# The projection of v and the second product of g in native float32

## The chip, the cores and the metric

One core of a Trainium2 chip runs the kernel. The metric is the device time of one execution in microseconds (us), as the median of several runs. Beside the timed runs there is one profiled execution, and all rows below come from it.

## The reference, cut to what matters

The kernel computes two layers, each a token mixer and a SwiGLU feed-forward network with post-normalisation, on x of 256 tokens by 1024 channels in float32. The first mixer is an RWKV-7 time mixing; the change touches v and g in it:

```
xx = time_shift(x) - x
xr, xw, xk, xv, xa, xg = [x + xx * mu[n] for n in range(6)]
r, k, v = xr @ w_r, xk @ w_k, xv @ w_v        # 256x1024 @ 1024x1024
g = sigmoid(xg @ g1) @ g2                     # g1: 1024x160, g2: 160x1024
...
S = S * w_t + (S @ -kk_t) b_t^T + v_t k_t^T   # per head and token
y_t = S @ r_t
y = group_norm(y) * gn_g + gn_b + bonus * v
return (y * g) @ w_o
```

The recurrence over tokens is done in four chunks of 64 tokens: the scores within a chunk, the inverse of a triangular matrix of each head and chunk, then four dependent steps (z, u, s, y) from chunk to chunk.

## The kernel before, in words

Most products are made from split parts. A weight piece of 128x1024 is loaded into a raw buffer (three of them in a ring), ScalarE (ACT) casts it to float32r as its high part (`hi`), and VectorE (DVE) or GpSimd (POOL) subtracts that from the raw piece to get the low part (`lo`); `PL` names the pieces whose subtraction is on POOL. The activations are split likewise (`xhi`, `xlo`). A product is then three matmuls: hi by xhi, lo by xhi, hi by xlo. `Stream` does this for every weight in the order of `weight_specs`; a piece of kind "native" is loaded into a slot of its own and used as float32 without a split (the first two pieces of k and both of g1), "stack" splits into one tile whose row groups hold hi, hi and lo, and "keep" leaves the parts in slots. All weight loads are issued by SyncE (SP), in that order.

In the first layer PE computes k, then r, then the scores (`sc`) of the chunks, the transposed keys (`bkt`), the bonus sums, the first half of v's columns, g1 and g2, and v's second half. v has the activations as the stationary side and 512 columns of the weights as the moving side: two halves of columns by two halves of tokens by 8 pieces of channels, 32 products. v's second half is cut into 16 units of one product. FREE = 10 of them run as they can; the rest are handed out one by one as fills for PE, four inside `merge` (counts in FILLI), and the last two in the recurrence (`fill`).

xv and xg are mixed on POOL (MIXV, MIXG), as two multiplications and additions on 128x512 for each quarter. xv is then split, by casts on ACT and subtractions on POOL ("xxv" in OFF); xg isn't, as g1 is native. The sigmoid of g's first product, `hg`, is split on ACT and DVE: three row groups, so that g2 takes four matmuls of 256 columns for each 128 channels, on stacked copies of the last 32 rows.

`inverse` runs on DVE: four transposes LT<-SC, a loop of 31 steps in which each product (`tmp<-LT,TT`) and addition (`TT<-TT,tmp`) needs the one before, then transposes TN and SC<-TT. `merge` multiplies the blocks on PE (n, t) with copies on ACT in between, and `recurrence` starts with z.

The order of the work is made in the program by `Issue`, a list of parts with ranks that are run against modelled times (`Clock`), and then by the framework's scheduler on each engine. After the mixer come the output projection, the networks and the attention, whose weights run through the same stream.

Of the kernel before, what the change touches and what calls it, by code (L numbers as in the profile page):

```python
# [8 lines left out]
F32 = mybir.dt.float32  # L9
# [7 lines left out]
T = 256  # L17
# [48 lines left out]
BON = 'pool'  # L66
BONW = 'T'
ORDERED = False
PL = {'wo1': [5, 6, 7], 'in1': [0, 1, 2, 3], 'qkv': [1, 3, 4, 5, 6, 7, 11], 'wo0': [1, 2, 4, 6, 7, 9, 10], 'k': [2], 'r': [0], 'v': [2, 3, 4, 5, 6, 7], 'g2': [0, 1], 'w2': [], 'in0': [0, 2, 3, 5]}
LD = {}  # L70
MIXV = 'pool'
MIXG = 'pool'
# [25 lines left out]
ORDER = mybir.DependencyInfo(mybir.DependencyClass.NoSync, mybir.DependencyReason.DATA)  # L98


class Stream:


# [8 lines left out]
        self.used = [Event() for _ in range(len(specs) + 1)]  # L112

    def load(self, upto):
        while self.nl < len(self.specs) and (self.nl < upto or self.specs[self.nl][1] == "native"):
            i = self.nl
            name, kind, a, b, rows, src = self.specs[i]
            if kind == "native":
                raw = self.slot([1024], f"nat{i}")
            else:  # L120
                raw = self.wp.tile([128, 1024], F32, tag="raw", name=f"raw{i}", bufs=RAW)
            v = raw[:rows, :a * b].rearrange("p (a b) -> p a b", a=a)
            if kind != "native":
                self.ring.append(i)
                if len(self.ring) > RAW:
                    self.I.clk.floor = max(self.I.clk.floor, self.freed.get(self.ring[-RAW - 1], 0.0))
            self.sync.dma_start(v, src.rearrange("p (a b) -> p a b", a=a))
            self.raw[i] = v
            self.nl += 1

    def run(self):
        for i, (name, kind, a, b, rows, src) in enumerate(self.specs):
            if i > 0 and self.specs[i - 1][1] == "raw":
                yield self.used[i]
            self.load(i + RAW)
            lead = self.lead.get(i, SPL - 1)
            if i >= lead:
                yield self.used[i - lead]
            r = self.raw.pop(i)
            if kind in ("native", "raw"):  # L140
                self.sp[i] = r
                self.I.reach(self.split[i], r)
                continue
            hl = []
            for t in ("hi", "lo")[:1 if kind in ("stack", "cast") else 2]:
                if kind in ("keep", "cast"):
                    x = self.slot([1024], f"{t}{i}", F32R)
                else:
                    x = self.wp.tile([128, 1024], F32R, tag=t, name=f"{t}{i}", bufs=SPL)
                hl.append(x[:rows, :a * b].rearrange("p (a b) -> p a b", a=a))  # L150
            if kind in ("split", "stack") and i >= SPL:
                yield self.done[i - SPL]
            if i in self.hold:
                yield self.hold[i]
            if name in self.gates:
                yield self.gates[name]
            yield r
            if kind in ("stack", "cast"):
                (self.pool.tensor_copy if kind == "cast" else self.act.copy)(out=hl[0], in_=r)
                yield hl[0]  # L160
                x = slice(rows // 3 * 2, rows)
                if kind == "stack":
                    (self.pool if i in self.pooled else self.dve).tensor_tensor(hl[0][x], r[x], hl[0][x].bitcast(F32), ALU.subtract)
                self.freed[i] = self.I.clk.ready(hl[0])
                self.sp[i] = hl
                self.I.reach(self.split[i], hl[0])
                continue
            n = 2 if name == "wo0" else 1
            c = b // n
            for j in range(n):  # L170
                self.act.copy(out=hl[0][:, :, j * c:(j + 1) * c], in_=r[:, :, j * c:(j + 1) * c])
                yield hl[0][:, :, j * c:(j + 1) * c]
                (self.pool if i in self.pooled else self.dve).tensor_tensor(hl[1][:, :, j * c:(j + 1) * c], r[:, :, j * c:(j + 1) * c],
                                       hl[0][:, :, j * c:(j + 1) * c].bitcast(F32), ALU.subtract)
            self.freed[i] = self.I.clk.ready(hl[1])
            self.sp[i] = hl
            self.I.reach(self.split[i], hl[1])
# [194 lines left out]
def weight_specs(a):  # L372
# [3 lines left out]
    def s1(name, key, idx, kind="split", cols=128):  # L376
        specs.append((name, kind, KT, cols, 128, a[key][idx]))

    def s2(name, key, cb, kind="split"):
        for q in range(4):  # L380
            specs.append((name, kind, 2, 512, 128, a[key][cb * 4 + q]))
# [18 lines left out]
            specs.append(("sel", "cast", KT, 128, 48, a["selT"]))  # L400
    for p in range(KT):
        s1("r", "w_r", p)
    s2("v", "w_v", 0)
    s1("g1", "w_g1a", 0, "native")
    s1("g1", "w_g1b", 0, "native", 96)
    specs.append(("g2", "split", 1, 1024, 128, a["w_g2a"]))
    specs.append(("g2", "stack", 1, 1024, 96, a["w_g2b"]))
    s2("v", "w_v", 1)
    s2("wo0", "w_o0", 0)
    s2("wo0", "w_o0", 1, "keep")  # L410
    s2("wo0", "w_o0", 0)
# [11 lines left out]
def trunk(ctx, tc, a, out):  # L423
# [23 lines left out]
    def slot(shape, name, dtype=F32):  # L447
        return tp.tile([128] + shape, dtype, tag="t4", name=nm(name))
# [4 lines left out]
    def half_slot(name, dtype=F32):  # L453
        return sm.tile([128, 2, T], dtype, tag="w2", name=nm(name), bufs=6)
# [4 lines left out]
    def ev(name):  # L459
        return E.setdefault(name, Event())  # L460
# [9 lines left out]
    def mm(ps, lhsT, rhs, start, stop, **kw):  # L470
        pe.matmul(ps, lhsT, rhs, start=start, stop=stop, **kw)
# [726 lines left out]
    def v_part(ps, w, hf, q, kks=(0, 1)):  # L1198
        for kk in kks:
            k = q * 2 + kk  # L1200
            xh, xl = mixed["xv"][k // 4]
            for n, (ww, xx) in enumerate(((w[0], xh), (w[1], xh), (w[0], xl))):
                mm(ps, xx[:, k % 4, TOK[hf]], ww[:, kk, :], start=(k + n == 0), stop=(k + n == KT + 1))

    def v_done(hf, cb, ps):
        act.copy(out=vt[hf][:, cb * 512:(cb + 1) * 512], in_=ps)
# [4 lines left out]
        I.reach(ev(f"v{cb}{hf}"), vt[hf][:, cb * 512:(cb + 1) * 512],  # L1211
                *(x[:, :, cb * 4:cb * 4 + 4] for x in UV[2 * hf:2 * hf + 2]))

    hgs = slot([3, T], "hg", F32R)

    def gates(n, rows, ps):

        yield ps[:rows, :T]
        x = half_slot("sg")[:rows, 0, :]
        act.activation(x, ps[:rows, :T], AF.Sigmoid)  # L1220
        yield x
        act.copy(out=hgs[:rows, n * 2, :], in_=x)
        yield hgs[:rows, n * 2, :]
        if n == 0:
            dve.tensor_tensor(hgs[:, 1, :], x, hgs[:, 0, :].bitcast(F32), ALU.subtract)
        else:
            dve.tensor_tensor(hgs[32:64, 2, :], x[32:64], hgs[32:64, 2, :].bitcast(F32), ALU.subtract)
        I.reach(ev(f"hg{n}"), hgs[:rows, n:n * 2 + 1, :] if n else hgs[:, 0:2, :])

    def g_done(u, ps):  # L1230
        act.copy(out=gT[u // 2][:, (u % 2) * 2:(u % 2) * 2 + 2, :], in_=a2(ps))
# [3 lines left out]
    def dense0():  # L1235
# [30 lines left out]
        for q in range(4):  # L1266
            ps = bank("r")
            for j in range(2):
                w = yield from W.get("r")
                yield from mm_s1(ps[:, j * T:(j + 1) * T], w, mixed["xr"])  # L1270
            I.add(3, receptance(q, ps))
            if q == 2:
                mix(3, "xv", 3, slot, eng=dict(pool=pool, dve=dve)[MIXV])
        early.close()
        scp = l0.enter_context(tc.tile_pool(name="scp", bufs=1))
        SC = scp.tile([128, 2, KT, NC, 128], F32, name="SC")
# [10 lines left out]
        for hf in range(2):  # L1287
            I.after(ps[hf], v_done, hf, 0, ps[hf])
        yield ev("xg")
        for n, rows in enumerate((128, 96)):  # L1290
            w = yield from W.get("g1")
            ps = bank("g1")
            for k in range(KT):
                mm(ps[:rows, :T], w[:, k, :], mixed["xg"][k // 4][:, k % 4, :], start=(k == 0), stop=(k == KT - 1))
            I.add(1, gates(n, rows, ps))
            yield 0.0
# [4 lines left out]
        for u in range(4):  # L1301
            ps = bank("g")
            for j in range(2):
                p = u * 2 + j
                for n, (ww, xx_) in enumerate(((g2[0][0], hgs[:, 0, :]), (g2[0][1], hgs[:, 0, :]), (g2[0][0], hgs[:, 1, :]),
                                               (g2[1][0], hgs[:96, 2, :]))):
                    mm(ps[:, j * T:(j + 1) * T], ww[:, 0, p * 128:(p + 1) * 128], xx_, start=(n == 0), stop=(n == 3))
                yield 0.0
            I.after(ps, g_done, u, ps)
        ws = []  # L1310
# [377 lines left out]
def _layout(inp):  # L1688
# [3 lines left out]
    def s1(w, n=128):  # L1692
        return w.reshape(KT, 128, w.shape[1] // n, n).transpose(2, 1, 0, 3).reshape(w.shape[1] // n, 128, KT * n)
# [10 lines left out]
    d["w_r"], d["w_k"], d["w_v"] = s1(rkv[0]), s1(rkv[1]), s2(rkv[2])  # L1704
    d["w_1"] = np.concatenate([inp["rwkv_w1"][0], inp["rwkv_a1"][0]], axis=1).reshape(2, 4, 128, 128).transpose(0, 2, 1, 3).reshape(2, 128, 512)
    d["w_2"] = np.stack([np.concatenate([w, w], axis=0) for w in (inp["rwkv_w2"][0], inp["rwkv_a2"][0])])
    d["w_g1a"], d["w_g1b"] = s1(inp["rwkv_g1"][0][:, :128]), s1(np.tile(inp["rwkv_g1"][0][:, 128:], (1, 3)), 96)
    d["w_g2a"], d["w_g2b"] = inp["rwkv_g2"][0][:128], np.tile(inp["rwkv_g2"][0][128:], (3, 1))
    d["w_o0"], d["w_o1"], d["w_qkv"] = s2(inp["rwkv_w_o"][0]), s2(inp["moba_w_o"][0]), s2(inp["moba_w_qkv"][0])
    for i in range(2):  # L1710
        w = inp["ffn_w_in"][i].reshape(KT, 128, 2, NJ, 128).transpose(3, 2, 1, 0, 4)
# [30 lines left out]
```

## Time and profile before

| | before |
|---|---|
| runs | 755.3, 751.78, 755.85 us; median 755.3 |
| profiled execution | 752.51 us, span from first to last instruction 750.7 us |
| mean granted PE clock | 0.963 |
| busy: PE, DVE, ACT, POOL | 692.8, 512.6, 359.3, 185.0 us |
| DMA | 117.27 MB, mean 156 GB/s |
| shares of the chain that ended last | PE 66%, DVE 10%, DMA 2% |

Times in rows are in us from the start of the span, durations of single instructions in ns where the view says so. PE is the matmul side of TensorE and PEld its weight loads. A matmul's duration in the rows is longer than the distance to the next one, because matmuls are pipelined; the distance between starts is what a matmul costs in a sequence. The granted clock of a stretch is a share of 2.4 GHz, so that 0.5 stands for 1.2 GHz. Nearly all instructions carry line 300, that of a helper, so that rows are told apart by their tiles. A native float32 matmul of the program stands as two instructions in the rows.

### The profile page before, as it was taken

To read this page: it belongs to the slowest core of one execution; us is meant where nothing else is said; L and a number is where in the kernel's file an instruction comes from. 1 tells how busy PE (TensorE), PEld (TensorE's weight loads), DVE (VectorE), ACT (ScalarE), POOL (GpSimd) and SP (SyncE) were. 2 spreads that over 40 slices of the span, in tenths; PEclk is the share of its full clock that TensorE was granted. 3 is DMA by queue.
4 is the path that set the end of the run, shared out by engine and by line. 5 is a ranking of instruction groups with operands and counts; after the bars stand their busy time and mean duration, and the time that the engine had idled before them with its cause. 6 is when DMAs were issued, how large, how long until landed. Compare 5 with 4: busy or idle time off the path is not lost.

```text
span 750.7 us, 12852 instructions
## 1 busy us (share of the span) xinstructions
PE 692.8 (92%) x5140; PEld 620.0 (83%) x5140; DVE 512.6 (68%) x827; ACT 359.3 (48%) x591; POOL 185.0 (25%) x132
## 2 busy tenths in 40 slices
PE   6899795798789999999999799999979999999996
PEld 5899784677668999999999578777769999999995
DVE  7989989938897655455555945876685554554566
ACT  5873234356545444434446314756635444444450
POOL 5667973333373000000000623113040000000000
PEclk9999998779999999999999989999999999999998
DMA  6445312110566655555557615445055555565551
GB/s 240 151 143 188 101 62 85 57 58 31 186 196 194 213 183 194 176 191 189 179 193 219 209 49 169 140 141 196 29 169 191 175 195 187 180 195 177 189 169 56
DMA packets 33580, 117.27 MB, mean 156 GB/s; under 512 B 3809, under 2 KB 4833, under 8 KB 33521
## 3 DMA queue, kind: packets, MB, share of 16 engines
q1 hardware_dynamic: 31936, 110.89, 45.3%
q10 hardware_dynamic: 1584, 5.57, 2.4%
q8 instruction: 40, 0.66, 0.4%
q14 instruction: 20, 0.16, 0.1%
HBM read 115.40 MB, written 1.05 MB: 155 GB/s over the span
## 4 chain that ended last, share of the span: by engine, by line
PE 66%; DVE 10%; DMA 2%; ACT 1%; issue 1%; DVEq 0%; ACTq 0%
PE gu L300 30%; PE acc L300 14%; PE qkv L300 9%; DVE xtok L300 4%; PE o L300 3%; PE gn L300 2%; DMA raw<-in_w_qkv_dram 2%; PE v L300 1%; PE tr L300 1%; DVE sc L300 1%; PE n L300 1%; PE ptr L300 1%; PE pv L300 1%; DVE lo L300 1%; PE att L300 1%
## 5 line engine op out<-in xcount | busy, mean ns | idle before, releaser
L300 DVE TENSOR_TENSOR lo<-raw,hi 128x1024 fp32r<-128x1024 f32 (+1 forms) x172 | 209.9, 1225 | 162.7 <-ACT hi L300 162.5
L300 ACT CAST hi<-raw 128x1024 fp32r<-128x1024 f32 (+1 forms) x214 | 212.4, 1001 | 209.1 <-PE gu L300 83.1
L300 PE MATMUL gu<-xhi,hi 128*128 128x256 f32 x640 | 181.1, 283 | 0.0
L300 PE MATMUL gu<-xlo,hi 128*128 128x256 f32 x640 | 181.0, 283 | 0.0
L300 PE MATMUL gu<-xhi,lo 128*128 128x256 f32 x640 | 180.9, 283 | 0.0
L300 POOL TENSOR_TENSOR lo<-raw,hi 128x1024 fp32r<-128x1024 f32 (+1 forms) x41 | 88.4, 2172 | 260.0 <-ACT hi L300 255.4
L300 PEld LDWEIGHTS gu<-xhi,hi 128*128 128x128 f32 x640 | 121.7, 190 | 0.7
L300 PEld LDWEIGHTS gu<-xhi,lo 128*128 128x128 f32 x640 | 121.7, 190 | 0.7
L300 PEld LDWEIGHTS gu<-xlo,hi 128*128 128x128 f32 x640 | 121.7, 190 | 0.0
L300 PE MATMUL acc<-hi,hl 128*128 128x512 f32 (+1 forms) x180 | 53.7, 368 | 0.0
L300 PE MATMUL acc<-lo,hh 128*128 128x512 f32 (+1 forms) x180 | 53.6, 367 | 0.0
L300 PE MATMUL acc<-hi,hh 128*128 128x512 f32 (+1 forms) x180 | 53.5, 367 | 0.0
L300 PE MATMUL qkv<-hi,xhi 128*128 128x512 f32 x96 | 40.6, 423 | 2.4 <-ACT xhi L300 2.4
L300 ACT CAST hh<-silu 128x256 fp32r<-128x256 f32 x40 | 16.2, 406 | 49.4 <-DVE silu L300 49.4
L300 PE MATMUL qkv<-lo,xhi 128*128 128x512 f32 x96 | 39.6, 412 | 0.0
L300 PE MATMUL qkv<-hi,xlo 128*128 128x512 f32 x96 | 39.6, 412 | 0.0
L300 PEld LDWEIGHTS acc<-hi,hl 128*128 128x128 f32 x180 | 32.8, 188 | 5.9
L300 PEld LDWEIGHTS acc<-lo,hh 128*128 128x128 f32 x180 | 32.7, 188 | 5.7
L300 PEld LDWEIGHTS acc<-hi,hh 128*128 128x128 f32 x180 | 31.8, 189 | 4.6
L300 PE MATMUL o<-hi,xhi 128*128 128x512 f32 x64 | 27.2, 425 | 3.0 <-ACT xhi L300 3.0
L300 DVE TENSOR_TENSOR hl<-silu,hh 128x256 fp32r<-128x256 f32 x40 | 17.0, 425 | 17.4 <-ACT hh L300 17.4
L300 PE MATMUL o<-hi,xlo 128*128 128x512 f32 x64 | 26.4, 415 | 0.0
(225 smaller groups left out, 1289.3 us busy)
## 6 DMA issues: line engine op xcount, KB each, us to landing
raw<-in_w_in_dram SPq DMA_DIRECT2D x80, 512.0 KB, 3.5
raw<-in_w_dn_dram SPq DMA_DIRECT2D x44, 512.0 KB, 3.5
raw<-in_w_qkv_dram SPq DMA_DIRECT2D x24, 512.0 KB, 3.9
raw<-in_w_o_dram SPq DMA_DIRECT2D x20, 512.0 KB, 3.6
raw<-in_w_r_dram SPq DMA_DIRECT2D x8, 512.0 KB, 3.9
raw<-in_w_v_dram SPq DMA_DIRECT2D x8, 512.0 KB, 3.5
raw<-in_w_if_dram SPq DMA_DIRECT2D x8, 512.0 KB, 3.4
raw<-in_w_k_dram SPq DMA_DIRECT2D x6, 512.0 KB, 3.8
```

What stands on the lines that cost most here:

```text
L300: ins = f(*args, **kw).ins
```

## The change

The four pieces of v's first half stay in the raw ring as loaded ("raw"); the four of its second half and the two of g2 are loaded straight into buffers of the rings that hold hi and lo parts ("in lo", "in hi"). xv is mixed into plain float32 tiles and not split. hg is written by the sigmoid alone. Each product of v becomes one native float32 matmul instead of three, each of g2 two (128 and 32 rows) instead of four. The last 32 rows of g1 and g2 are no longer repeated three times.

```diff
--- before.py
+++ after.py
@@ -66,7 +66,7 @@
 BON = 'pool'
 BONW = 'T'
 ORDERED = False
-PL = {'wo1': [5, 6, 7], 'in1': [0, 1, 2, 3], 'qkv': [1, 3, 4, 5, 6, 7, 11], 'wo0': [1, 2, 4, 6, 7, 9, 10], 'k': [2], 'r': [0], 'v': [2, 3, 4, 5, 6, 7], 'g2': [0, 1], 'w2': [], 'in0': [0, 2, 3, 5]}
+PL = {'wo1': [5, 6, 7], 'in1': [0, 1, 2, 3], 'qkv': [1, 3, 4, 5, 6, 7, 11], 'wo0': [1, 2, 4, 6, 7, 9, 10], 'k': [2], 'r': [0], 'in0': [0, 2, 3, 5]}
 LD = {}
 MIXV = 'pool'
 MIXG = 'pool'
@@ -98,6 +98,9 @@
 ORDER = mybir.DependencyInfo(mybir.DependencyClass.NoSync, mybir.DependencyReason.DATA)
 
 
+NATIVE = ("native", "in hi", "in lo")
+
+
 class Stream:
 
 
@@ -112,15 +115,17 @@
         self.used = [Event() for _ in range(len(specs) + 1)]
 
     def load(self, upto):
-        while self.nl < len(self.specs) and (self.nl < upto or self.specs[self.nl][1] == "native"):
+        while self.nl < len(self.specs) and (self.nl < upto or self.specs[self.nl][1] in NATIVE):
             i = self.nl
             name, kind, a, b, rows, src = self.specs[i]
             if kind == "native":
                 raw = self.slot([1024], f"nat{i}")
+            elif kind in NATIVE:
+                raw = self.wp.tile([128, 1024], F32R, tag=kind[3:], name=f"nat{i}", bufs=SPL).bitcast(F32)
             else:
                 raw = self.wp.tile([128, 1024], F32, tag="raw", name=f"raw{i}", bufs=RAW)
             v = raw[:rows, :a * b].rearrange("p (a b) -> p a b", a=a)
-            if kind != "native":
+            if kind not in NATIVE:
                 self.ring.append(i)
                 if len(self.ring) > RAW:
                     self.I.clk.floor = max(self.I.clk.floor, self.freed.get(self.ring[-RAW - 1], 0.0))
@@ -137,7 +142,7 @@
             if i >= lead:
                 yield self.used[i - lead]
             r = self.raw.pop(i)
-            if kind in ("native", "raw"):
+            if kind in NATIVE + ("raw",):
                 self.sp[i] = r
                 self.I.reach(self.split[i], r)
                 continue
@@ -400,12 +405,12 @@
             specs.append(("sel", "cast", KT, 128, 48, a["selT"]))
     for p in range(KT):
         s1("r", "w_r", p)
-    s2("v", "w_v", 0)
+    s2("v", "w_v", 0, "raw")
     s1("g1", "w_g1a", 0, "native")
-    s1("g1", "w_g1b", 0, "native", 96)
-    specs.append(("g2", "split", 1, 1024, 128, a["w_g2a"]))
-    specs.append(("g2", "stack", 1, 1024, 96, a["w_g2b"]))
-    s2("v", "w_v", 1)
+    s1("g1", "w_g1b", 0, "native", 32)
+    specs.append(("g2", "in hi", 1, 1024, 128, a["w_g2a"]))
+    specs.append(("g2", "in hi", 1, 1024, 32, a["w_g2b"]))
+    s2("v", "w_v", 1, "in lo")
     s2("wo0", "w_o0", 0)
     s2("wo0", "w_o0", 1, "keep")
     s2("wo0", "w_o0", 0)
@@ -1198,9 +1203,7 @@
     def v_part(ps, w, hf, q, kks=(0, 1)):
         for kk in kks:
             k = q * 2 + kk
-            xh, xl = mixed["xv"][k // 4]
-            for n, (ww, xx) in enumerate(((w[0], xh), (w[1], xh), (w[0], xl))):
-                mm(ps, xx[:, k % 4, TOK[hf]], ww[:, kk, :], start=(k + n == 0), stop=(k + n == KT + 1))
+            mm(ps, mixed["xv"][k // 4][:, k % 4, TOK[hf]], w[:, kk, :], start=(k == 0), stop=(k == KT - 1))
 
     def v_done(hf, cb, ps):
         act.copy(out=vt[hf][:, cb * 512:(cb + 1) * 512], in_=ps)
@@ -1211,21 +1214,13 @@
         I.reach(ev(f"v{cb}{hf}"), vt[hf][:, cb * 512:(cb + 1) * 512],
                 *(x[:, :, cb * 4:cb * 4 + 4] for x in UV[2 * hf:2 * hf + 2]))
 
-    hgs = slot([3, T], "hg", F32R)
+    hgs = slot([2, T], "hg")
 
     def gates(n, rows, ps):
 
         yield ps[:rows, :T]
-        x = half_slot("sg")[:rows, 0, :]
-        act.activation(x, ps[:rows, :T], AF.Sigmoid)
-        yield x
-        act.copy(out=hgs[:rows, n * 2, :], in_=x)
-        yield hgs[:rows, n * 2, :]
-        if n == 0:
-            dve.tensor_tensor(hgs[:, 1, :], x, hgs[:, 0, :].bitcast(F32), ALU.subtract)
-        else:
-            dve.tensor_tensor(hgs[32:64, 2, :], x[32:64], hgs[32:64, 2, :].bitcast(F32), ALU.subtract)
-        I.reach(ev(f"hg{n}"), hgs[:rows, n:n * 2 + 1, :] if n else hgs[:, 0:2, :])
+        act.activation(hgs[:rows, n, :], ps[:rows, :T], AF.Sigmoid)
+        I.reach(ev(f"hg{n}"), hgs[:rows, n, :])
 
     def g_done(u, ps):
         act.copy(out=gT[u // 2][:, (u % 2) * 2:(u % 2) * 2 + 2, :], in_=a2(ps))
@@ -1270,7 +1265,7 @@
                 yield from mm_s1(ps[:, j * T:(j + 1) * T], w, mixed["xr"])
             I.add(3, receptance(q, ps))
             if q == 2:
-                mix(3, "xv", 3, slot, eng=dict(pool=pool, dve=dve)[MIXV])
+                mix(3, "xv", 3, eng=dict(pool=pool, dve=dve)[MIXV])
         early.close()
         scp = l0.enter_context(tc.tile_pool(name="scp", bufs=1))
         SC = scp.tile([128, 2, KT, NC, 128], F32, name="SC")
@@ -1287,7 +1282,7 @@
         for hf in range(2):
             I.after(ps[hf], v_done, hf, 0, ps[hf])
         yield ev("xg")
-        for n, rows in enumerate((128, 96)):
+        for n, rows in enumerate((128, 32)):
             w = yield from W.get("g1")
             ps = bank("g1")
             for k in range(KT):
@@ -1302,9 +1297,8 @@
             ps = bank("g")
             for j in range(2):
                 p = u * 2 + j
-                for n, (ww, xx_) in enumerate(((g2[0][0], hgs[:, 0, :]), (g2[0][1], hgs[:, 0, :]), (g2[0][0], hgs[:, 1, :]),
-                                               (g2[1][0], hgs[:96, 2, :]))):
-                    mm(ps[:, j * T:(j + 1) * T], ww[:, 0, p * 128:(p + 1) * 128], xx_, start=(n == 0), stop=(n == 3))
+                for n, rows in enumerate((128, 32)):
+                    mm(ps[:, j * T:(j + 1) * T], g2[n][:, 0, p * 128:(p + 1) * 128], hgs[:rows, n, :], n == 0, n == 1)
                 yield 0.0
             I.after(ps, g_done, u, ps)
         ws = []
@@ -1704,8 +1698,8 @@
     d["w_r"], d["w_k"], d["w_v"] = s1(rkv[0]), s1(rkv[1]), s2(rkv[2])
     d["w_1"] = np.concatenate([inp["rwkv_w1"][0], inp["rwkv_a1"][0]], axis=1).reshape(2, 4, 128, 128).transpose(0, 2, 1, 3).reshape(2, 128, 512)
     d["w_2"] = np.stack([np.concatenate([w, w], axis=0) for w in (inp["rwkv_w2"][0], inp["rwkv_a2"][0])])
-    d["w_g1a"], d["w_g1b"] = s1(inp["rwkv_g1"][0][:, :128]), s1(np.tile(inp["rwkv_g1"][0][:, 128:], (1, 3)), 96)
-    d["w_g2a"], d["w_g2b"] = inp["rwkv_g2"][0][:128], np.tile(inp["rwkv_g2"][0][128:], (3, 1))
+    d["w_g1a"], d["w_g1b"] = s1(inp["rwkv_g1"][0][:, :128]), s1(inp["rwkv_g1"][0][:, 128:], 32)
+    d["w_g2a"], d["w_g2b"] = inp["rwkv_g2"][0][:128], inp["rwkv_g2"][0][128:]
     d["w_o0"], d["w_o1"], d["w_qkv"] = s2(inp["rwkv_w_o"][0]), s2(inp["moba_w_o"][0]), s2(inp["moba_w_qkv"][0])
     for i in range(2):
         w = inp["ffn_w_in"][i].reshape(KT, 128, 2, NJ, 128).transpose(3, 2, 1, 0, 4)
```

## Rows read from the trace of the kernel before

**Rows 1.** Stages: busy time per engine, granted PE clock, DMA share, GB/s.
```profile
81.00:99.00 18.00, 14.98 (x155) 14.41 (x154) 16.27 (x23) 5.12 (x8) 17.84 (x14) 0.91 0.35 110
121.30:130.10 8.80, 0.56 (x4) 0.33 (x2) 8.77 (x44) 0.78 (x2) 0.00 (x0) 0.74 0.18 61
130.10:136.40 6.30, 6.24 (x30) 5.99 (x31) 6.24 (x36) 1.49 (x3) 0.00 (x0) 0.55 0.00 0
136.40:148.20 11.80, 7.91 (x86) 6.38 (x84) 11.65 (x21) 5.10 (x9) 6.68 (x6) 0.91 0.28 90
148.20:160.00 11.80, 11.80 (x108) 9.01 (x106) 7.93 (x6) 4.82 (x10) 1.04 (x1) 0.52 0.00 0
```

**Rows 2.** The chain of waits: start us, duration us, what.
```profile
143.25 1.92 DVE TN L300
...
166.25 0.61 PE z L300 x16
...
263.93 5.74 PE gu L300 x48
```

**Rows 3.** Timeline of DVE: start us, duration us, engine, line, operation, out<-in, count.
```profile
70.92 0.67 DVE L300 TENSOR_TENSOR KB<-kkr,a 64x512 f32<-64x512 f32 x1
...
78.64 2.34 DVE L300 TENSOR_TENSOR lo<-raw,hi 128x1024 fp32r<-128x1024 f32 x2
...
81.50 2.86 DVE L300 TENSOR_TENSOR KB<-k,E 64x512 f32<-64x512 f32 x2
...
84.39 1.65 DVE L300 TENSOR_TENSOR KB<-kkr,a 64x512 f32<-64x512 f32 x1
...
99.22 2.09 DVE L300 STREAM_TRANSPOSE LT<-SC 32x1024 f32<-32x1024 f32 x1
...
110.45 2.50 DVE L300 TENSOR_TENSOR tmp<-LT,TT 128x135 f32<-128x135 f32 x1
112.99 0.30 DVE L300 TENSOR_TENSOR TT<-TT,tmp 128x135 f32<-128x135 f32 x1
...
129.69 0.42 DVE L300 TENSOR_TENSOR hg<-sg,hg 128x256 fp32r<-128x256 f32 x1
...
137.46 0.29 DVE L300 TENSOR_TENSOR tmp<-LT,TT 128x32 f32<-128x32 f32 x2
137.69 2.50 DVE L300 TENSOR_TENSOR TT<-TT,tmp 128x32 f32<-128x32 f32 x2
140.10 2.50 DVE L300 TENSOR_TENSOR tmp<-LT,TT 128x16 f32<-128x16 f32 x2
```

**Rows 4.** Timeline of POOL.
```profile
75.65 6.46 POOL L300 TENSOR_TENSOR xlo<-mx,xhi 128x512 fp32r<-128x512 f32 x1 [0.56 <-POOL KB L300]
...
83.89 4.51 POOL L300 TENSOR_TENSOR xlo<-mx,xhi 128x512 fp32r<-128x512 f32 x3
...
93.95 2.03 POOL L300 TENSOR_TENSOR mix<-xx,vec 128x512 f32<-128x512 f32 x2
...
100.23 2.32 POOL L300 TENSOR_TENSOR mix<-mix,xT 128x512 f32<-128x512 f32 x2
...
110.41 2.39 POOL L300 TENSOR_TENSOR hi<-raw,hi 32x1024 fp32r<-32x1024 f32 x1 [2.24 <-ACT hi L300]
...
137.73 4.74 POOL L300 TENSOR_TENSOR lo<-raw,hi 128x1024 fp32r<-128x1024 f32 x2 [16.80 <-ACT hi L300]
```

**Rows 5.** Timeline of PE at v's first half and g1.
```profile
106.11 0.48 PE L300 MATMUL v<-hi,xhi 128*128 128x512 f32 x1
...
114.31 0.40 PE L300 MATMUL v<-hi,xlo 128*128 128x512 f32 x1
114.56 7.07 PE L300 MATMUL g<-mix,nat 128*128 128x256 f32 x32
```

**Rows 6.** Waits: who waited for whom, us in total, times, longest.
```profile
PE g L300 <- DVE hg L300: 8.3, 1, 8.3
```

**Rows 7.** DMA issues: count, KB each, median us to landing.
```profile
raw<-in_w_v_dram SPq DMA_DIRECT2D x8, 512.0 KB, 3.5
```

## The prediction

> **What bounds the kernel now.** I first cut the span into stages by the granted clock and the idle time of PE, then followed the chain of waits backward through the stage in which v and g are computed, then read DVE and POOL in that stage in order of time. From about 248 us the two feed-forward networks and the attention run on PE nearly without a gap, at full clock; there the change touches nothing. What it touches lies between 65 us (the weights of v arrive) and 171 us (the last matmul of v).
>
> In that stage PE isn't the limit. From 81.0 (last matmul of r) to 166.2 (first matmul of the recurrence, z) the stage table [rows 1] shows PE idle for 18.00 - 14.98 = 3.0 us in the stretch from 81, 8.2 us in that from 121.3 and 3.9 us in that from 136.4. Its clock is 0.55 (near the 1.2 GHz level) in the stretch from 130.1, 0.91 in that from 136.4 and 0.52 in that from 148.2, each with idle time ahead of it; the busy time times what the clock lacks is 2.8 + 0.7 + 5.7 us. Together PE loses 24.3 us of 85.2. DVE is busy for 16.27 of 18.00, 8.77 of 8.80 and 11.65 of 11.80 us where PE idles.
>
> The chain says the same: it enters this stage from DVE, with the transposes TN at 143.25 that end the triangular inverse, goes over n, t and pieces of v on PE, and reaches z at 166.25 [rows 2]. So DVE sets the time until 143, PE from there to 166.
>
> Why is DVE late? Read its rows in the inverse against POOL's [rows 3, 4]. A product of 128x135 takes 2.50 us at 110.45, and its partner of the same shape 0.30 us at 112.99. POOL's subtraction for g2 runs from 110.41 for 2.39 us: DVE's instruction, issued 0.04 us later, ends just after it. The same happens under two subtractions that fill 137.73 to 142.47, at 137.69 and 140.10 (2.50 us for pairs; the pair at 137.46 takes 0.29). These POOL instructions make the low parts of the weights that the change no longer splits.
>
> **The change part by part.**
>
> DVE inside the inverse. POOL runs five such subtractions there: one of g2b, four of v (the pair at 137.73 is two of them). Each holds one DVE instruction for 2.50 less its own 0.30, so 2.2 us; five times that is 11.0 us. All of it goes. The two subtractions that made hg's low parts sit in DVE's order between the loop's instructions (one row stands at 129.69; the next loop instruction starts 0.33 us after it): together 0.8 us. Sum 11.8 us, all on the chain, as DVE has no idle time in the inverse. Ends: 11.8 at most; at least 11.8 - 8.6 = 3.2, if POOL's products for xg (four pairs that fill 93.95 to 102.55 [rows 4]) slide under the loop. I take the upper end, since POOL has nothing left to do ahead of xg once xv has no low part, and so xg should come earlier, not later.
>
> DVE ahead of the inverse. Two splits of v go, 2.34 us at 78.64. Two KB products at 81.50 take 2.86 and one at 84.39 takes 1.65, where the same form took 0.67 at 70.92 [rows 3]; xv's low parts are on POOL then (four, 6.46 + 4.51 us [rows 4]). The excess is 1.5 + 1.0 = 2.5 us. The upper end is 4.8 us, the lower 0: the scores follow r's last matmul on PE, and r's end doesn't move. Between them I take 3.5: I read PE's 3.0 us of idle time in the stretch from 81 [rows 1] as a wait for DVE to empty PSUM, but xg's products will take some of xv's place beside KB. With this the transposes LT start at 95.7 rather than 99.2 [rows 3], and the inverse ends at 143.2 - 3.5 - 11.8 = 127.9, so 15.3 us earlier.
>
> PE. A native matmul of 256 columns is two instructions; g1 shows 32 of them in 7.07 us, 0.221 each, 0.442 a matmul [rows 5]. With 512 columns no row exists. It lies between 0.44 (no dearer than 256 columns) and 0.96 us (two of the 0.48 that one 512-column instruction shows at 106.11), so 32 of them move PE by -8 to +9 us; by columns it is 0.87 to 0.88, and I take 0.87, since the row nearest in kind is g1's. Three matmuls on the split parts of v take 3 x 0.231 = 0.693 us (36 rows, starts 106.11 to 114.31, with 0.12 us lost at the first [rows 5]). So v's 32 products cost 32 x 0.177 = +5.7 us of PE. g2: 32 matmuls become 16 native ones, 16 x 0.442 = 7.1; the 32 at full clock would be 32 x 0.12 = 3.8 (48 of gu in 5.74 us [rows 2]): +3.3 us. Narrower g1 saves nothing, as both groups of g1 have 256 columns. Of the 9.0 us, 8.6 lie ahead of z: 16 products for v's first half, 14 for its second (the 4 forced as fills during the merges come after the 10 free ones), and g2.
>
> Do DVE's 15.3 us carry over to z? PE's floor: 85.2 - 24.3 (idle and half clock) + 8.6 = 69.5 us after 81.0, so z can start at 150.5 at the earliest, 15.7 us sooner. DVE's own limit is looser: TN at 128, the transposes back some 12 us later, about 140. So what is late next is PE, with v's second half: when the inverse ends at 128, PE has only just finished g2. It won't be without any wait: g2 still waits for the sigmoid, and n and t for copies on ACT. I put that at 2.5 us; the gain is 15.7 - 2.5 = 13.2 us. PE's 8.3 us wait for hg [rows 6] goes wholly, because hg now comes straight from ACT. With PE busy from 81 on, the half-clock stretches have no idle time ahead of them.
>
> The rest. ACT loses 16 casts, on no chain here. Raw buffers of v's first half are now freed by its matmuls instead of a split, so the fourth load of v waits on SP for the first one's matmuls, with g1, g2 and v's second half queued behind it, and after them w_o. Two products' worth of buffers (some 7 us of PE) cover its landing of 3.5 us [rows 7]; if that cover is gone the cost is under 4 us, and it falls on PE, which I bound at 0 to 4 and take as 0. Two slots fewer for xv cost nothing. Behind z, recurrence, output projection and networks are unchanged, and w_o's splits wait for v's buffers as before, so they move along.
>
> Sum against the profiled execution: 752.5 - 13.2 = 739.3 us. That execution stood 2.8 us under the median of the runs shown (755.3); the same gain from there gives 742.1. I say 741.
>
> **The rivals.**
>
> A. PE is the next bound sooner. The front gain is 0 (PE, not DVE, times the scores), and PE still has idle time, so it falls to half clock while v's products lie between n and t: 7 of them at 0.87 us more. The gain is 13.2 - 6 = 7 us: 748 from the median. For it: half clock after every gap in [rows 1]. Against it: a gap needs an engine that PE waits for, and hg's, the longest, is gone. Chance 0.25.
>
> B. POOL's work comes back, but only xg's. 15.3 - 8.6 = 6.7 us remain of DVE's gain; the last 7.7 of v's 16 products stay at half clock, each 1.74 against 1.39 us, so 2.7 us are lost: a gain of 4.0, 751.3 from the median, at the edge of no change. Chance 0.11, in which a change that does nothing at all (w_o's splits setting the time behind z anyway) is included.
>
> C. Slower. The inverse starts earlier, and w_o's raw loads need no split of v ahead of them, so besides xg's products w_o's POOL splits could also land under it. With four as long as v's, 2.37 us [rows 4]: 15.3 - 8.6 - 9.5 = -2.8, and 2.7 us for v at half clock: 5.5 us later, 760.8 from the median. It decides from about 12.6 us of POOL time under the loop (15.3 less 2.7). Against it: w_o's low parts need the buffers that v's second half holds until PE has used them, and PE gets there after 128. Chance 0.07. The Trainium skill speaks for this side (SBUF — State Buffer, Who interferes with whom): a DVE instruction with two SBUF inputs shuts out, or is shut out by, a GpSimd instruction that reads SBUF, for the whole instruction, while one with at most one SBUF input is untouched. The trace agrees on both kinds so far: 2.50 us at 110.45 for two inputs, and 2.09 us for the transpose at 99.22 [rows 3], which has one input, lies under xg's products, and is little longer than TN's 1.92 [rows 2]. By that rule xg's products cost DVE nothing where they lie now, and their full length under the loop.
>
> **How the numbers follow.** Forecast 0.54 (736 to 745), A 0.25 (745 to 751), B 0.11 (751 to 757), C 0.07, and 0.03 for a gain beyond PE's floor, from a shorter stretch ahead of 81. No change means within 0.5% of 755.3, so 751.5 to 759.1; less can't be told from noise here. Faster 0.54 + 0.25 + 0.03 = 0.82, same 0.11, slower 0.07. The range 734 to 752 leaves out C, most of B and the best case.
>
> **What would show it.** Right: no DVE instruction of the loop above 0.6 us but those under the bonus products; LT to TN shorter by 11 to 12 us; PE clock 1.0 between 115 and z; a native pair of v at 0.87 us; z near 153. Wrong: POOL rows of 1 us or more under the loop; idle PE between 100 and 150; z moved earlier with the networks' first matmul not following; or a native v product far from 0.87.

## The result, and the profile after

The changed kernel takes 757.92 us (median of 20 runs, 754.4 to 759.77); the kernel before took 753.67 us on the same chip. The ratio of the two is 1.0061 [1.0043, 1.0078]: slower by 0.6%, where 741 us was forecast. The profiled execution has a span of 757.1 us and took 758.9; its mean granted clock is 0.956 (before 0.963).

First DVE and POOL, for which the gain was claimed. DVE's timeline of the kernel after (start us, duration us, engine, line, operation, out<-in, count):

```profile
77.06 3.06 DVE L305 TENSOR_TENSOR KB<-k,E 64x512 f32<-64x512 f32 x2
80.15 1.42 DVE L305 TENSOR_TENSOR KB<-kkr,a 64x512 f32<-64x512 f32 x1
...
93.55 7.84 DVE L305 STREAM_TRANSPOSE LT<-SC 32x1024 f32<-32x1024 f32 x4
...
114.97 1.33 DVE L305 TENSOR_TENSOR TT<-TT,tmp 128x224 f32<-128x224 f32 x2
...
124.86 0.28 DVE L305 TENSOR_TENSOR tmp<-LT,TT 128x16 f32<-128x16 f32 x2
...
125.47 3.79 DVE L305 STREAM_TRANSPOSE TN<-TT 32x1024 f32<-32x1024 f32 x2
```

and POOL's of the same kernel, from the end of xg on:

```profile
92.68 2.34 POOL L305 TENSOR_TENSOR mix<-mix,xT 128x512 f32<-128x512 f32 x2
112.21 1.60 POOL L305 TENSOR_TENSOR v<-v,sb 128x512 f32<-128x512 f32 x1 [17.19 <-ACT v L305]
115.19 1.08 POOL L305 TENSOR_TENSOR v<-v,sb 128x512 f32<-128x512 f32 x1 [1.38 <-ACT v L305]
...
```

LT starts at 93.55 instead of 99.22 [rows 3], TN at 125.47 instead of 143.25 [rows 2]. From LT to TN it is 31.9 us instead of 44.0. Where a pair took 2.50 us at 140.10 [rows 3], it takes 0.28; POOL has nothing under the loop but two products for the bonus and a few copies; the product at 115.19 is seen in DVE's 1.33. So the inverse ends 17.8 us sooner, and yet z starts 6 us later. What PE does with that time is in its timeline:

```profile
100.96 12.26 PE L305 MATMUL v<-raw,mix 128*128 128x512 f32 x28
113.06 7.19 PE L305 MATMUL g<-mix,nat 128*128 128x256 f32 x32
127.50 3.59 PE L305 MATMUL n<-TN,SC 32*32 32x32 f32 x64 [7.25 <-DVE TN L305]
131.02 2.37 PE L305 MATMUL g<-hg,nat 128*128 128x256 f32 x4
133.32 3.62 PE L305 MATMUL n<-TN,SC 32*32 32x32 f32 x64
136.86 16.17 PE L305 MATMUL g<-hg,nat 128*128 128x256 f32 x28
152.96 12.19 PE L305 MATMUL v<-nat,mix 128*128 128x512 f32 x22
165.09 2.21 PE L305 MATMUL t<-SC,TN 32*32 32x32 f32 x64
```

PE stands idle for 7.25 us for TN, while g2, whose inputs are there (with the order changed it starts right behind g1, as the first experiment shows), is behind n in its order. Then n takes 3.59 us where at full clock it takes 2.21 (t, of the same form, at 165.09), and 28 of g2's 32 matmul instructions take 16.17 us, 0.578 each, where the forecast had 0.221. The stretches of the kernel after (length, busy us and count of PE, PEld, DVE, ACT and POOL, granted clock, DMA share, GB/s) show one cause for both:

```profile
80.40:96.60 16.20, 16.20 (x185) 15.36 (x184) 16.16 (x23) 4.18 (x8) 14.35 (x14) 1.00 0.34 121
96.60:100.00 3.40, 3.40 (x6) 1.66 (x7) 3.37 (x3) 0.00 (x0) 0.00 (x0) 0.50 0.00 0
...
120.00:127.50 7.50, 0.25 (x3) 0.03 (x2) 7.36 (x35) 0.37 (x1) 2.83 (x5) 0.76 0.00 0
127.50:137.00 9.50, 9.50 (x133) 8.07 (x133) 9.38 (x5) 1.76 (x4) 0.00 (x0) 0.50 0.01 3
137.00:153.00 16.00, 16.00 (x29) 6.89 (x29) 0.08 (x1) 4.15 (x8) 1.46 (x3) 0.50 0.00 0
153.00:158.00 5.00, 5.00 (x7) 2.15 (x7) 0.00 (x0) 3.25 (x7) 0.00 (x0) 0.50 0.00 0
158.00:172.00 14.00, 14.00 (x151) 8.03 (x149) 1.29 (x2) 4.71 (x10) 3.52 (x3) 1.00 0.13 41
```

The clock falls to the 1.2 GHz level in the idle stretch and stays there from 127.5 to 158, though PE is busy in every us of it. That is 30.5 us at half clock; before it was chiefly 6.30 us at 0.55 and 11.80 at 0.52 [rows 1]. A shorter stretch at half clock, from 96.6 to 100, has no idle time ahead of it: PE is busy in every us from 80.4 on.

Behind z the chain of waits of the kernel after (start us, duration us, what) loses a little more:

```profile
172.40 0.61 PE z L305 x16
...
212.70 4.73 POOL lo L305 x3
...
217.45 3.43 DMA raw<-in_w_o_dram
...
273.63 5.60 PE gu L305 x48
```

z starts 6.15 us later than in [rows 2], and the networks' 48 gu of [rows 2] 9.7 us later (273.63 for 263.93): 3.55 us more are lost between the two, where the chain goes over POOL's low parts of w_o and the load behind them; no run tests which of its rows costs them. The two executions differ by 6.4 us (758.9 for 752.5), so the networks give some 3.3 us back. No run tells what makes them shorter; their 48 gu take 5.60 us for 5.74.

### The profile page after: what moved, and what is told of

Same layout as the page of the kernel before. It is cut to its first block, busy times and chain, and to the rows that moved or that the text cites. A ratio compares the mean times of both kernels' runs of the same rounds, so it can differ in the third digit from the quotient of the medians.

```text
span 757.1 us, 12739 instructions
## 1 busy us (share of the span) xinstructions
PE 705.6 (93%) x5108; PEld 607.8 (80%) x5108; DVE 497.1 (66%) x823; ACT 346.0 (46%) x575; POOL 153.5 (20%) x120
## 4 chain that ended last, share of the span: by engine, by line
PE 66%; DVE 19%; DMA 5%; ACT 4%; issue 3%; POOL 2%; DVEq 0%; SPq 0%; ACTq 0%; POOLq 0%
PE gu L305 29%; PE acc L305 14%; PE qkv L305 9%; DVE xtok L305 3%; PE g L305 2%; PE v L305 2%; DVE lo L305 2%; PE gn L305 2%; DVE TT L305 2%; DVE tmp L305 2%; POOL lo L305 2%; PE o L305 2%; DMA raw<-in_w_qkv_dram 1%; ACT hi L305 1%; DVE SC L305 1%
## 5 line engine op out<-in xcount | busy, mean ns | idle before, releaser
L305 DVE TENSOR_TENSOR lo<-raw,hi 128x1024 fp32r<-128x1024 f32 (+1 forms) x170 | 205.5, 1212 | 185.9 <-ACT hi L305 158.4
L305 ACT CAST hi<-raw 128x1024 fp32r<-128x1024 f32 (+1 forms) x204 | 202.4, 999 | 198.2 <-PE gu L305 90.9
L305 POOL TENSOR_TENSOR lo<-raw,hi 128x1024 fp32r<-128x1024 f32 (+1 forms) x34 | 70.8, 2100 | 242.3 <-ACT hi L305 223.3
L305 PE MATMUL o<-lo,xhi 128*128 128x512 f32 x64 | 26.3, 414 | 0.6 <-POOL lo L305 0.6
```

The lines of the kernel that those rows point to most:

```text
L305: ins = f(*args, **kw).ins
```

## The experiments

All are built on the kernel after, unless it is said otherwise, and their ratios are to the kernel before. The median of the kernel before lies between 752.2 and 754.0 us in the groups of runs that the ratios come from, so a difference of two experiments in us is good to some 2 us. The theory formed from the profile: the gain on DVE is real, and PE's fixed order throws it away, by what it leaves idle, and by the clock behind that.

**Order alone.** n waits in PE's order for all of g2.

```diff
         yield ev(f"TN{hp}")
+        yield ev("g2d")
...
             I.after(ps, g_done, u, ps)
+        I.reach(ev("g2d"))
```

> Changed kernel, with the blocks n of the merge held in the program's order until g2's products are issued; same work. Theory: in the changed kernel PE stood idle from 120.2 to 127.5 us, because n, which waits for DVE's TN, was ahead of g2 in PE's fixed order; its clock then stayed at 1.2 GHz until 158, and g2, n and the first products of v ran there. With g2 in the gap the clock stays at 2.4 GHz, z starts near 151 rather than 172.4 and the kernel takes 735 to 743 us. Rival 1, native products are too dear for PE in any order: only the 7.3 us of idle time come back, z near 165, 749 to 752 us. Rival 2, the loss lies behind z (output projection, weights of the networks): z comes earlier and the time stays at 755 to 758.

743.52 us, 0.9855 [0.9797, 0.9912]: 14.4 us less than the kernel after by one edit of order, at the edge of the theory's range. PE's timeline:

```profile
124.50 9.71 PE L305 MATMUL g<-hg,nat 128*128 128x256 f32 x32
134.13 3.21 PE L305 MATMUL n<-TN,SC 32*32 32x32 f32 x64
...
158.52 0.68 PE L305 MATMUL z<-UV,SC 64*64 64x64 f32 x16
```

There is no idle time left ahead of n, but z comes at 158.5 and not near 151. g2 takes 9.71 us, 0.303 an instruction, and two stretches of the same kernel, over g2 and behind it, show that this is at full clock:

```profile
124.50:134.10 9.60, 9.60 (x33) 4.88 (x32) 9.40 (x14) 3.84 (x8) 2.99 (x6) 1.00 0.00 0
134.10:139.00 4.90, 4.90 (x67) 3.92 (x67) 4.13 (x3) 2.89 (x6) 1.00 (x2) 0.57 0.00 0
```

So a second thing is wrong with g2 itself, and behind it the clock falls once more, for a shorter time. It is also 0.50 from 97.2 to 107.5, ahead of the rows shown, with PE busy throughout.

**The idle time filled.** Needless matmuls of 128x128x256 behind g1, on a copy of a mask, with the order left as it is.

```diff
...
+        ps = bank("idle")
+        for _ in range(DUM):
+            mm(ps[:, :T], wk[:, :128], wk, True, True)
```

> Changed kernel in its own order, with 56 needless float32r matmuls of 256 columns (some 6.3 us) behind g1, in the gap in which PE stood idle. Nothing useful is done sooner. Theory (it is the clock that costs): n starts at 127.5 as before, but n, g2 and v run at 2.4 GHz, z starts near 157, 740 to 747 us. Rival (it is the idle time and the order alone that cost): z stays near 172, 756 to 759 us.

759.24 us, 1.0113 [1.0077, 1.0149]; no gain, and z at 171.6, as the rival has it. With DUM = 56 PE still waits 1.73 us for TN, and the clock is 0.50 from 130 to 156. A shorter gap didn't keep the clock; whether it was the gap or the matmuls behind it this run can't tell.

**One part of the change at a time.** First v alone, with g2 and hg split as before:

```diff
+    specs.append(("g2", "split", 1, 1024, 128, a["w_g2a"]))
+    specs.append(("g2", "stack", 1, 1024, 96, a["w_g2b"]))
...
+        dve.tensor_tensor(hgs[:, 1, :], x, hgs[:, 0, :].bitcast(F32), ALU.subtract)
```

> Only v native; g2 and the sigmoid split as before the change. n stays ahead of most of g2 in PE's order, so the gap and the fall of the clock stay. Theory (g2's native products at 1.2 GHz, 0.58 us for each of 32, are most of the loss; v's leave 1.2 GHz sooner): z near 160, 744 to 750 us. Rival (v's native products keep PE slow): z at 168 or later, 753 to 758 us.

747.68 us, 0.9907 [0.9873, 0.9942], as the theory has it, although PE waits even longer for TN here:

```profile
129.51 3.59 PE L305 MATMUL n<-TN,SC 32*32 32x32 f32 x64 [8.57 <-DVE TN L305]
```

Then g2 alone, with v split as before:

```diff
-    s2("v", "w_v", 0, "raw")
+    s2("v", "w_v", 0)
...
+            for n, (ww, xx) in enumerate(((w[0], xh), (w[1], xh), (w[0], xl))):
```

> Only g2 native; v split as before the change, with its POOL subtractions under the inverse. g2 stands ahead of n here. Theory: PE's wait for the low part of hg goes, one POOL subtraction (2.2 us) and two DVE subtractions (0.8 us) leave the inverse, g2 runs at 2.4 GHz: 749 to 753 us. Rival (native g2 is itself the loss): 755 to 760 us.

757.55 us, 1.0039 [1.0002, 1.0076], as the rival has it. So by itself v's half of the change is worth 0.9% and g2's costs some 0.4%. That would make 0.995 for the two, and 1.0061 was measured: the idle time alone doesn't make the kernel slower than before (v_only has it too), but the idle time with g2's native matmuls behind it does. Two stretches of g2_only, in the first of which g2's matmuls begin at 122.60, right behind g1's:

```profile
122.60:125.20 2.60, 2.60 (x10) 1.55 (x10) 2.60 (x15) 0.37 (x1) 0.00 (x0) 1.00 0.68 205
125.20:136.30 11.10, 11.10 (x24) 4.82 (x23) 11.07 (x63) 1.75 (x3) 0.00 (x0) 0.60 0.00 0
```

Here the clock falls while PE is busy without a break, in the middle of g2.

**g2's price.** g2's matmuls alternate between one of 128 contracted rows and one of 32; g1's all have 128. Padding the second part with zeros to 128 (and the second group of g1's columns, which makes its rows) makes them alike, with as many instructions as without:

```diff
-    s1("g1", "w_g1b", 0, "native", 32)
+    s1("g1", "w_g1b", 0, "native")
...
-        for n, rows in enumerate((128, 32)):
+        for n, rows in enumerate((128, 128)):
...
+    d["w_g2a"], d["w_g2b"] = inp["rwkv_g2"][0][:128], np.pad(inp["rwkv_g2"][0][128:], ((0, 96), (0, 0)))
```

> Changed kernel in its own order (n ahead of most of g2), with the second, 32-row part of g1 and g2 padded with zeros to 128 columns and rows: same number of matmuls, all of them 128x128 by 256. Theory now: g2's native matmuls that alternate between 128 and 32 rows are slow (0.29 us each at 2.4 GHz, 0.58 at 1.2 GHz, where g1's take 0.22) and leave the array so little to do that the clock stays at 1.2 GHz. Padded, each takes 0.22 us at 2.4 GHz and 0.43 at 1.2 GHz, the clock comes back within some 14 us of n's start, and z comes 5 to 8 us earlier: 749 to 753 us. Rival (it is native float32, not the rows, that is slow at 1.2 GHz and keeps the clock there): 0.5 us or more each, z within 2 us of the changed kernel's, 756 to 759 us.

747.94 us, 0.9931 [0.9901, 0.9961]: 10 us less than the kernel after, with PE's order unchanged, and better than the theory had it. PE waits 5.82 us for TN, the clock falls as before, but it comes back sooner:

```profile
127.20:141.30 14.10, 14.10 (x144) 12.15 (x145) 9.45 (x5) 2.89 (x5) 1.46 (x3) 0.50 0.01 1
```

That is 14.1 us at half clock behind the gap for 30.5 with the alternating rows. Both edits together:

> Both: g2's products ahead of n in PE's order, and padded to 128 rows. Theory: g2 takes 7.1 us rather than 9.7, the clock doesn't fall at its end, z at 153 to 156 rather than 158.5: 737 to 742 us. Rival (only the order mattered): z at 158, 742 to 745 us.

733.95 us, 0.9744 [0.9679, 0.9809], on four executions: faster than both kernels, and under the forecast and the theory's range. PE's timeline of the kernel with both:

```profile
115.39 7.07 PE L305 MATMUL g<-mix,nat 128*128 128x256 f32 x32
122.30 7.07 PE L305 MATMUL g<-hg,nat 128*128 128x256 f32 x32
129.30 2.21 PE L305 MATMUL n<-TN,SC 32*32 32x32 f32 x64
...
150.65 0.68 PE L305 MATMUL z<-UV,SC 64*64 64x64 f32 x16
```

and its stretches over g2, n and v:

```profile
120.00:130.00 10.00, 10.00 (x66) 8.61 (x65) 9.86 (x40) 4.69 (x11) 3.63 (x7) 1.00 0.00 0
130.00:140.00 10.00, 10.00 (x127) 6.29 (x125) 8.00 (x5) 5.58 (x12) 0.51 (x2) 1.00 0.01 2
```

g2 costs exactly what g1 does, 0.221 an instruction, as forecast, and PE works at full clock through n, t and v. z starts at 150.65; the forecast's floor for it was 150.5. That agreement is luck in part: from 98.0 to 104.8 the clock is 0.50 with PE busy, and without these 6.8 us z would come some 3.4 us ahead of the floor.

A third form keeps the 32 rows but issues all products of 128 rows first and then all of 32 (in the better order):

```diff
+        gs = [bank("g") for _ in range(4)]
+        for n, rows in enumerate((128, 32)):
+            for u in range(4):
+                for j in range(2):
...
-                for n, rows in enumerate((128, 32)):
```

> g2's products ahead of n; not padded, but all eight 128-row products first and then all eight with 32 rows, so that the row count changes once instead of 15 times. If the alternation is what costs: 0.22 us each in both groups, and as padded, 737 to 742 us. If a 32-row native matmul is itself slow: 0.22 for the first group, 0.35 for the second, 742 to 745 us.

744.49 us, 0.9871 [0.979, 0.9952]. Its 16 instructions of 128 rows run from 121.80 to 125.44, and the 16 of 32 rows from there to 129.72:

```profile
121.80:125.44 3.64, 3.64 (x17) 2.95 (x16) 3.64 (x20) 0.37 (x1) 2.20 (x4) 1.00 0.00 0
125.44:128.40 2.96, 2.96 (x15) 2.55 (x15) 2.82 (x5) 2.29 (x5) 1.02 (x2) 1.00 0.00 0
128.40:129.70 1.30, 1.30 (x4) 0.58 (x2) 1.30 (x1) 0.93 (x2) 0.00 (x0) 0.50 0.00 0
```

With the last 1.3 us, at half clock, counted half, the second block takes 3.6 us like the first: sixteen 32-row matmuls in a row cost what sixteen 128-row ones do, and the price lies in changing from one to the other. But the clock falls inside the second block and stays at 0.50 until 145.5, and the time stays that of order alone: in the range of the second theory, for another reason. What in a row of 32-row matmuls brings the clock down is not shown.

**Does the gain need a free POOL?** Padding with v still split as before:

> Only g2 native, padded to 128 rows; v split as before the change, so POOL's subtractions stay under the inverse and TN stays at 137. Theory: g2 takes 7.1 us instead of 13.8, but PE only waits longer for n (until 139): z within 1.5 us of the unpadded kernel's 163.4, 753 to 758 us; so v's relief of POOL and DVE is what the gain needs. Rival (g2's native price alone made that kernel slow): 6 us or more earlier, 747 to 751 us.

757.5 us, 1.0059 [1.0028, 1.0089]. Its g2 takes 7.07 us from 123.31 at full clock, and PE then waits 10.26 us for TN: the cheaper g2 only makes the wait longer, for POOL's splits of v hold DVE as they did before. And the opposite test, on order alone: five needless POOL subtractions of 128x1024 put under the loop.

```diff
...
+            for _ in range(5):
+                pool.tensor_tensor(scr, LT.rearrange("p a b -> p (a b)"), scr, ALU.subtract)
```

> g2's products ahead of n, and five needless subtractions of 128x1024 on POOL beneath the inverse's loop on DVE, behind xg's products; everything else as in the kernel with g2 ahead of n. Theory: each holds one DVE instruction for 2.2 us, so TN starts 11 us later, at 137 to 138 rather than 126.6; PE then waits for n, so z is at 164 to 168 and the time 749 to 755 us. Rival (DVE's gain came from something else than POOL's instructions): TN moves by under 2 us and the time stays at 742 to 745 us.

750.27 us, 0.9961 [0.9922, 0.9999], 6.8 us more than order alone (1.1% by the ratios), as the theory has it. POOL's row:

```profile
101.73 12.36 POOL L305 TENSOR_TENSOR scr<-LT,scr 128x1024 f32<-128x1024 f32 x5 [5.76 <-DVE LT L305]
```

DVE's beside it:

```profile
101.91 2.28 DVE L305 TENSOR_TENSOR TT<-TT,tmp 128x31 f32<-128x31 f32 x1
...
111.75 2.46 DVE L305 TENSOR_TENSOR tmp<-LT,TT 128x112 f32<-128x112 f32 x1
...
136.13 3.83 DVE L305 STREAM_TRANSPOSE TN<-TT 32x1024 f32<-32x1024 f32 x2
```

Five DVE instructions are held to 2.28 to 2.46 us where they take 0.19 to 0.27 alone, and TN moves from 126.6 to 136.13. That is the mechanism of the forecast, put back by hand: TN 9.5 us later, 6.8 us in all.

**Gap or what follows it?** The padded kernel in its own order, with needless matmuls, first 50:

> As the padded kernel in the changed order (n ahead of most of g2), with 50 needless float32r matmuls of 256 columns (some 6.2 us) in PE's gap ahead of n. The first filled gap left 1.7 us open and g2's alternating rows in place; here neither is left. Theory (idle time brings the clock down, g2's alternating rows held it there): with both gone n, g2 and v run at 2.4 GHz, z at 156 to 157 against 161.7 without the filling, 741 to 744 us. Rival (n's small matmuls bring the clock down by themselves): z at 161 to 163, 747 to 750 us.

749.21 us, 0.9956 [0.993, 0.9983], no better than padding alone; they left a gap of 3.17 us, and the clock was 0.60 from 128 to 138. Then 80:

> The kernel with g2's second part padded to 128 rows and PE's order left as it is, with 80 instead of 50 needless matmuls behind g1, so that no idle time is left ahead of n (50 of them took 6.33 us and left 3.17 us). Theory that idle time ahead brings the clock down: granted clock 1.00 from 120 to 150, n 2.2 us for 64, g2 at 0.22 an instruction, z 154 to 156.5, 741 to 744.5 us. Rival, n's small matmuls with g2 behind them bring it down with no gap ahead: clock 0.50 from about 128 to 138 again, z 160 to 161, 748 to 750.

744.01 us, 0.9899 [0.9862, 0.9935]. PE's timeline of the latter:

```profile
123.06 9.93 PE L306 MATMUL idle<-wk 128*128 128x256 f32 x80
132.92 2.21 PE L306 MATMUL n<-TN,SC 32*32 32x32 f32 x64
135.06 1.13 PE L306 MATMUL g<-hg,nat 128*128 128x256 f32 x4
136.12 2.21 PE L306 MATMUL n<-TN,SC 32*32 32x32 f32 x64
138.26 6.31 PE L306 MATMUL g<-hg,nat 128*128 128x256 f32 x28
```

and one of its stretches:

```profile
130.00:140.00 10.00, 10.00 (x165) 9.22 (x165) 7.64 (x4) 2.88 (x5) 1.46 (x3) 1.00 0.01 2
```

With no gap n and g2 run at full clock in the same order in which they ran at half clock behind a gap. The two kernels differ in the number of needless matmuls alone, so with g2's rows alike it is the idle time ahead of n, not n's small matmuls, that brings the clock down here. The z expected at 154 to 156.5 came at 161.2, since an earlier stretch at 0.57 (97 to 108, with PE busy) had delayed g1's end to 123 and the needless matmuls ran on to 132.9. The profiled execution, 747.41 us, is the longest of the five; their median is in the range of the theory.

**v native, g2 split, in the better order.** Would g2's native form be needed at all? The split of v_only with n's wait of the first experiment:

> v native, g2 split as in the kernel before, and n made to wait in PE's order for the whole of g2. If order was the chief loss and g2's native form adds little once v is native: g2 takes 32 matmuls of 0.12 us, so 3.9 us against 7.07 for the padded native one, but its low part lies under DVE's loop once (2.2 us) and hg's two subtractions stand in DVE's order (0.8 us), so TN comes at 128 to 130 and z at 150 to 155: 734 to 740. Rival, the low parts of g2 and hg come too late: n waits for g2, idle PE ahead of it, clock 0.50 behind it, z 160 or later, 745 to 750.

746.04 us, 0.9928 [0.9898, 0.9958]. PE's timeline:

```profile
125.44 0.73 PE L305 MATMUL g<-hg,hi 128*128 128x256 f32 x4 [2.23 <-ACT hg L305]
128.50 3.62 PE L305 MATMUL n<-TN,SC 32*32 32x32 f32 x64 [2.33 <-DVE TN L305]
```

The wait stands in the code, but in PE's order only 4 of g2's 32 matmuls came ahead of n; the other 28 run from 149.42 on, the first of them released by POOL's low part of g2. So the question is not answered: the low part came too late, as the rival said, and what a timely split would give wasn't measured.

## Why the prediction was wrong

**DVE inside the inverse: right.** 11.8 us were forecast, 44.0 - 31.9 = 12.1 came. What POOL does to DVE is shown in both directions, by the change and by pool_under_loop. The Trainium skill (SBUF — State Buffer, Who interferes with whom) has a two-input DVE instruction and a GpSimd instruction that reads SBUF shut each other out for the whole instruction; five DVE rows of 2.28 to 2.46 us beside five POOL instructions of 12.36 / 5 = 2.47 us agree.

**DVE ahead of the inverse: undersized, and half of its reason wrong.** 3.5 us forecast, 99.22 - 93.55 = 5.7 measured, above the upper end of 4.8. But the excess of 2.5 us on the three KB products, half of that 4.8, did not go: they take 3.06 us at 77.06 and 1.42 at 80.15, for 2.86 and 1.65 [rows 3], now beside POOL's mixing. They start 4.4 us sooner; the two splits account for 2.3 of that, and the rest isn't traced. TN came at 125.5 instead of the 127.9 forecast.

**PE, the price of v: right.** A product of 512 columns takes 2 x 12.26 / 28 = 0.876 us at full clock (0.864 from start to start), for 0.87.

**PE, the price of g2: wrong.** 16 x 0.442 = 7.1 us were taken from g1's row, as if a native matmul of 256 columns cost the same whatever its neighbours. Alternating 128 and 32 rows they take 9.71 us at full clock (order alone), 2.6 more, and made alike 7.07. At half clock it is 0.578 each. The weight loads, first of order alone and then of the kernel with both edits, show where matmuls of different rows meet:

```profile
126.18 0.30 PEld L305 LDWEIGHTS g<-hg,nat 128*128 128x128 f32 x2 [0.33 <-issue]
...
123.81 1.70 PEld L305 LDWEIGHTS g<-hg,nat 128*128 128x128 f32 x8
```

With alternating rows two loads come together and then none for 0.33 us; with rows alike eight follow one another. What in the engine makes them pause isn't shown. In g2_only the same matmuls also let the clock fall with no gap ahead, which cost 13.75 us for 32 instead of 9.71.

**"When the inverse ends at 128, PE has only just finished g2": the step that failed first.** TN ended on time, even early; g2 hadn't begun. The forecast took PE's order as work that is done when its inputs are ready. The order is fixed when the program is built, and in the kernel after it put half of n's matmuls ahead of all of g2, and the other half ahead of 28 of its 32 instructions. In the kernel before g2 stood in front of n, and so PE's longest wait there was the 8.3 us for hg [rows 6]. The change took that wait away and brought one of 7.25 us for TN, ahead of work that was ready.

**"With PE busy from 81 on, the half-clock stretches have no idle time ahead of them": failed with it.** There was a gap, and the stretch behind it was at half clock. Closing the gap gave 1.00 for 0.60 (gap_closed_padded against filled_gap_padded), so that much of the rule it rests on held. The rest didn't: with PE busy the clock fell too, from 96.6 to 100 in the kernel after, in the middle of g2 in g2_only, and inside the 32-row block of the grouped form. Stretches like the first, of 3.4 to 10.3 us, begin near the end of the bonus sums (matmuls of two columns) in 8 of the 11 profiled kernels with native v and in none of the three with v split; what brings them about wasn't tested.

The miss in z adds up: 172.4 came for 153 forecast, 19.4 us, or 21.9 with the 2.5 us of waits that the forecast had. Idle time cost 7.25 us and g2's rows 2.6. The half clock from 127.5 to 158 cost some 14.1 us, from start to start: n 7.06 us for 4.28 at full clock, g2 18.40 for 9.63, v 5.04 for 2.5. That from 96.6 to 100 cost 1.7. This makes 25.6, and the floor of 150.5 was itself some 3.3 us too late, as the kernel with both edits shows. Some of that stands in [rows 1]: the sum leaves out the clock of 0.91 in the stretch from 81, 14.98 x 0.09 = 1.3 us. 25.6 - 3.3 is 22.3, within half a us. In time the two steps are worth 14.4 us (order alone), 10 (padding alone) and 24 (both), so to within their intervals they add up.

**Rivals.** The time that came lies in the range that the prediction gave to no change, 751.5 to 759.1, but by a gain and a loss of like size, which none of its rivals has. A named the mechanism, a gap and the half clock behind it, but put it at v's products, at 6 us. B and C, POOL's work under the loop, didn't happen: POOL's mixing of xv and xg ends at 95.0, and the loop begins at 101.5, as forecast.

**"Recurrence, output projection and networks are unchanged ... so they move along": off by 3.55 us** between z and the networks, on POOL's splits of w_o, with some 3.3 us given back behind them.

## What to carry to other kernels

When a change moves an engine's inputs, read the order in which the consumer will issue its work, not only when the inputs are ready: a gain of 17.8 us on DVE became a loss, because a wait stood ahead of work that was ready, and that work kept the clock low behind the wait. Price an instruction from rows of its own shape and its own neighbours. And look for the half-clock stretch behind each new gap: here a wait of 7.25 us cost some 14 us more with g2's alternating rows behind it, and one of 5.82 us some 7 (half of 14.1) with rows alike.

## What the runs showed of the hardware

- Native float32 matmuls of 128 and 32 contracted rows in turn take 0.303 us an instruction at full clock, against 0.221 for rows all alike. In two blocks, the 32-row ones cost no more than the 128-row ones (3.6 us for 16). Adding zeros to the shorter ones made the kernel faster by 10 us.
- The granted clock stayed at the 1.2 GHz level for 30.5 us with PE busy throughout (127.5 to 158), where with rows alike it came back after 14.1 us. It also fell inside busy stretches: in g2_only (1.00 up to 125.2, 0.60 behind it), and near the end of the bonus sums in the kernel after (0.50 from 96.6 to 100).
- Behind a gap of 3.17 us the clock was 0.60 over the next 10 us; with the gap filled by needless matmuls it was 1.00 over the same instructions.
